# A 2x2 block product by seven quarter products in the up-projection of a gated feed-forward layer, with the activations split at the down-projection

## The chip, the cores and the metric

One core of a Trainium2 chip. The time is the device time of one execution in microseconds. The profile is one further execution of the same program, taken by the hardware profiler. In its rows PE is TensorE, DVE is VectorE, ACT is ScalarE, POOL is GpSimd and SP the queue that issues most transfers.

## The reference

Two decoder layers on x of 512 tokens and 1024 channels, in float32: a mixer and a layer norm, then a gated feed-forward block and another layer norm. The change concerns the feed-forward block alone:

```
def conv_ffn(x, w_up, conv_w, conv_b, w_down):
    h = causal_dwconv(x @ w_up, conv_w, conv_b)
    val, gate = jnp.split(h, 2, axis=-1)
    return (jax.nn.silu(gate) * val) @ w_down
...
    for layer in range(DEPTH):
        ...
        f = conv_ffn(x, ffn_w_up[layer], ffn_conv_w[layer], ffn_conv_b[layer], ffn_w_down[layer])
        x = layer_norm(ALPHA * x + f, ln2_g[layer], ln2_b[layer])
```

D_FF is 2816, so w_up is 1024 x 5632 and w_down 2816 x 1024. The convolution is depthwise over time, with three taps.

## The kernel before

Precision. TensorE multiplies in fp32r. Each float32 operand is split into a high part, which is the operand rounded to fp32r, and a low part, the difference. A product is the sum of three: high x high, low x high, high x low. `split` (L284 to L286) makes the high part on ScalarE and the low part on VectorE, or on GpSimd where the call says so.

Up-projection. `ffn` goes over 22 channel groups j of 128 channels. For each group there is a block of weights for the gate and one for the value, 128 x 1024 floats or 512 KB each: eight sub-blocks of 128 x 128, one for each 128 channels of the input. `mtile` loads and splits a block (`wload`) and runs `mpass`: 24 matmuls with 512 columns (all tokens), three passes over eight sub-blocks, into one PSUM tile. `conv` then applies the three taps: ScalarE starts with scale and bias out of PSUM (L979), and VectorE adds the two shifted taps, reading PSUM and SBUF (L981). The gate goes through Silu (L988), VectorE multiplies (L990), and the result h is split into high and low part (low part on GpSimd). All 44 parts of h stay in SBUF.

Down-projection. `proj_ln` forms h x w_down with tokens on the partitions. It goes over 11 pairs b of groups, twice: once for each half of the 1024 output channels. A step b loads a block of weights and runs 24 matmuls with 512 columns, six for each of four token tiles (L330). In the second half the last four pairs (`nres`) stay loaded, and `last(t)` finishes one token tile after the other, so that the layer norm of a tile can begin. In layer 1 the last token tile is cut into two parts of 256 columns (`parts`).

Buffers. Weight blocks have a ring of four raw buffers (`raw`) and a ring of five pairs of high and low parts (`hi`, `lo`). PSUM has eight tiles: four `mm`, two `S`, one `tp`, one `av`. Feed-forward pools (`f0`, `f1`) are opened when the mixer's pool is closed, and the other way round.

Order. A planner of the language (a list of instructions for each engine, ordered by readiness and program order) sets the order on each engine; only the places named by the kernel (`issue_after`, the `Weave` class for the mixers) add to it. Nothing in the feed-forward stage is ordered by hand.

## Time and profile before

| | |
|---|---|
| runs | median 1183.83 us of 3 (1181.13 to 1184.2) |
| the profiled execution | 1183.14 us, span 1181.3 us, granted TensorE clock 0.993 |
| TensorE busy | 1156.3 us (98%) |
| VectorE busy | 691.6 us (59%) |
| ScalarE busy | 466.7 us (40%) |
| GpSimd busy | 193.7 us (16%) |

The span is what the profile covers; the time of the profiled execution is 1.8 us longer. Busy times of TensorE include the pipelining of its matmuls, so 98% busy doesn't mean that each matmul runs at the engine's peak.

### The profile page before, as it was taken

The numbers are of one execution on the slowest core, as the hardware profiler recorded it, in microseconds if no ns is written. First come the engines' busy times: TensorE is split into PE (matmuls) and PEld (weight loads), VectorE is DVE, ScalarE is ACT, GpSimd is POOL, SyncE is SP. The second block draws the span as 40 slices with busy tenths as digits, with TensorE's granted clock in tenths as the row PEclk, the third lists the DMA queues.
The fourth block names the chain that finished last, engine by engine and source line by source line (L and its number), as shares of the span: only waits on it lengthen the run. The fifth ranks groups of instructions, "written<-read, shape, count | busy, mean of one in ns | idle before, by whom it ended". The sixth has DMA issues, their size and how long they took to land.

```text
span 1181.3 us, 13893 instructions
## 1 busy us (share of the span) xinstructions
PE 1156.3 (98%) x5312; PEld 941.3 (80%) x5312; DVE 691.6 (59%) x1098; ACT 466.7 (40%) x715; POOL 193.7 (16%) x234
## 2 busy tenths in 40 slices
PE   8999999999999999999998999999999999999997
PEld 6867778887888888888887866687888888888886
DVE  5987756477555555542338888768555455542326
ACT  5445653224444444431214466614444444432110
POOL 1122222211101110100003048112110111110002
PEclk9999999999999999999999999999999999999999
DMA  8331341213222232233222242213222322242201
GB/s 301 111 108 72 108 158 58 98 45 133 99 91 105 89 107 90 103 130 106 90 72 81 89 143 90 98 63 107 91 105 90 107 90 101 96 139 93 96 30 72
DMA packets 37570, 119.79 MB, mean 101 GB/s; under 512 B 4200, under 2 KB 4840, under 8 KB 37504
## 3 DMA queue, kind: packets, MB, share of 16 engines
q1 hardware_dynamic: 37344, 118.38, 28.9%
q8 instruction: 42, 0.69, 0.2%
q0 software_dynamic: 160, 0.52, 0.2%
q14 instruction: 24, 0.20, 0.1%
HBM read 116.75 MB, written 2.15 MB: 101 GB/s over the span
## 4 chain that ended last, share of the span: by engine, by line
PE 91%; DVE 6%; POOL 1%; issue 1%; ACT 1%; DMA 0%; POOLq 0%; SPq 0%; DVEq 0%; ACTq 0%
PE mm L238 53%; PE mm L330 14%; PE S L330 7%; PE tp L330 3%; PE av L330 2%; PE mm L278 1%; PE S L261 1%; PE mm L427 1%; PE av L852 1%; DVE lo L286 1%; PE av L550 1%; DVE xk L411 1%; PE S L634 1%; PE tp L650 1%; PE tp L536 1%
## 5 line engine op out<-in xcount | busy, mean ns | idle before, releaser
L238 PE MATMUL mm<-xT,hi 128*128 128x512 f32 (+1 forms) x1984 | 491.3, 395 | 0.5 <-ACT xT L285 0.5
L238 PEld LDWEIGHTS mm<-xT,hi 128*128 128x128 f32 x1984 | 371.0, 189 | 80.1 <-issue 4.4
L286 DVE TENSOR_TENSOR lo<-raw,hi 128x1024 fp32r<-128x1024 f32 (+1 forms) x201 | 234.5, 1171 | 174.5 <-ACT hi L285 174.3
L285 ACT ACTIVATE hi<-raw 128x1024 fp32r<-128x1024 f32 (+1 forms) x203 | 202.3, 999 | 205.4 <-PE mm L330 133.7
L981 DVE SCALAR_TENSOR_TENSOR tmp<-mm,col,tmp 128x510 f32<-128x510 f32 (+1 forms) x176 | 131.3, 749 | 207.9 <-ACT tmp L979 205.0
L238 PE MATMUL mm<-xT,lo 128*128 128x512 f32 (+1 forms) x992 | 249.4, 390 | 0.0
L238 PEld LDWEIGHTS mm<-xT,lo 128*128 128x128 f32 x992 | 185.0, 188 | 38.6 <-issue 1.9
L286 POOL TENSOR_TENSOR h<-tmp,h 128x512 fp32r<-128x512 f32 x44 | 57.7, 1311 | 433.4 <-ACT h L285 433.4
L979 ACT ACTIVATE tmp<-mm,col 128x512 f32<-128x512 f32 x88 | 68.4, 779 | 129.7 <-PE mm L238 128.4
L330 PE MATMUL mm<-hi,h 128*128 128x512 f32 (+1 forms) x396 | 118.0, 378 | 0.0
L330 PEld LDWEIGHTS mm<-hi,h 128*128 128x128 f32 x396 | 73.6, 188 | 13.7
L330 PE MATMUL mm<-lo,h 128*128 128x512 f32 (+1 forms) x198 | 74.8, 378 | 0.0
L314 POOL TENSOR_SCALAR small<-small 128x1 f32<-128x1 f32 (+2 forms) x25 | 14.5, 580 | 341.0 <-DVE small L404 279.5
L285 ACT ACTIVATE h<-tmp 128x512 fp32r<-128x512 f32 x44 | 27.8, 632 | 100.1 <-DVE tmp L990 100.1
L330 PE MATMUL S<-hi,h 128*128 128x512 f32 x176 | 56.9, 390 | 0.0
L330 PEld LDWEIGHTS mm<-lo,h 128*128 128x128 f32 x198 | 37.3, 188 | 6.8
L330 PE MATMUL mm<-hi,T 128*128 128x512 f32 x128 | 42.4, 399 | 0.0
L285 ACT ACTIVATE xT<-mm 128x512 fp32r<-128x512 f32 x24 | 13.5, 596 | 66.6 <-PE mm L427 66.4
L988 ACT ACTIVATE tmp<-tmp 128x512 f32<-128x512 f32 x44 | 27.9, 633 | 28.8 <-DVE tmp L981 28.8
L330 PEld LDWEIGHTS S<-hi,h 128*128 128x128 f32 x176 | 33.1, 188 | 6.7
L330 PE MATMUL S<-lo,h 128*128 128x512 f32 x88 | 34.3, 390 | 0.0
L411 DVE SCALAR_TENSOR_TENSOR xk<-xk,small,tmp 128x512 f32<-128x512 f32 (+1 forms) x33 | 29.0, 922 | 6.0 <-POOL small L315 6.0
(233 smaller groups left out, 1236.2 us busy)
## 6 DMA issues: line engine op xcount, KB each, us to landing
raw<-in_W SPq DMA_DIRECT2D x190, 512.0 KB, 3.5
bc<-dr SPq DMA_DIRECT2D x20, 256.0 KB, 3.9
tmp<-in_rows SPq DMA_DIRECT2D x16, 256.0 KB, 4.0
raw<-in_W SPq DMA_DIRECT2D x8, 256.0 KB, 5.7
xk<-in_x SPq DMA_DIRECT2D x4, 512.0 KB, 5.8
tmp<-in_xT SPq DMA_DIRECT2D x7, 256.0 KB, 6.3
out<-xk SPq DMA_DIRECT2D x7, 256.0 KB, 2.0
kc<-in_consts SPq DMA_DIRECT2D x1, 352.0 KB, 6.2
```

The costliest lines, as they stand in the source:

```text
L238: T.matmul(o[:, :cols_], w[:, k * P:(k + 1) * P], xs_(xcur, part, k)[:, :cols_], start=n == 0, stop=n == 3 * NK - 1)
L261: T.matmul(os[t], xs_(xcur, part, k)[:, t * P:(t + 1) * P], w[:, sl], start=k == 0 and n == 0, stop=k == NK - 1 and n == 2)
L278: T.matmul(os[t], xs_(xcur, part, k)[:, t * P:(t + 1) * P], w[:, kk * 512:(kk + 1) * 512], start=b == 0 and kk == 0 and n == 0, stop=b == ...
L285: A.activation(hi, src, AF.Copy)
L286: (lo_eng or V).tensor_tensor(lo, src, r32(hi), ALU.subtract)
L314: G.tensor_scalar(dst, var, EPS, None, ALU.add)
L330: T.matmul(o[:, c], a[:, t * P:(t + 1) * P], ww[:, kk * 512 + c.start:kk * 512 + c.stop], start=first and kk == 0 and n == 0, stop=fin and ...
L411: V.scalar_tensor_tensor(z[:, c], z[:, c], rs, shift[h][:, c], ALU.mult, ALU.add)
L427: T.transpose(tp[:, k * P:(k + 1) * P], z[:, k * P:(k + 1) * P], ident)
L979: A.activation(c, o, AF.Identity, bias=c1(cb + j), scale=c1(cw + 2 * 2 * NJ + j))
L981: V.scalar_tensor_tensor(c[:, d:], o[:, :S - d], c1(cw + (2 - d) * 2 * NJ + j), c[:, d:], ALU.mult, ALU.add)
L988: A.activation(gt, gt, AF.Silu)
```

## The change

The up-projection of groups 0 and 1 stays. The other 20 groups are taken two at a time by `up_seven`. For a group, the gate block A and the value block B together with x form a 2x2 block product: the 1024 input channels are cut into two halves, the 512 tokens into two halves. The four quarters of the result (gate and value, left and right tokens) come from seven products of quarter size in place of eight: each is three passes over four sub-blocks with 256 columns, 12 matmuls (`mul`). For this, sums of weight blocks are formed for each group on GpSimd before they are split (`t`, and in place in `ra` and `rb`: four of 512 columns a group), and sums of quarters of x once a layer (E, S2, S3, S4, on VectorE and GpSimd). A pair of groups has seven splits of 1024 columns (one of them in two halves) instead of four; one low part is on GpSimd. The products are put together in SBUF tiles `g` and `v` by eight copies on ScalarE and eight sums of 256 columns on VectorE a pair; the convolution then reads `g` and `v`.

The product of gate and value moves from VectorE to GpSimd and is kept unsplit (`act`). The down-projection splits it where it is used, in both halves of the output, with the low part on GpSimd (`two`), in a ring of 11 tiles. That ring's pool (`dn`) is opened when the up-projection's pool (`up`) is closed.

The diff, without the lines of `proj_ln` that only pass `w` on:

```diff
--- before.py
+++ after.py
@@ -318,14 +318,18 @@
 
 
         nonlocal xcur
+        two = acts if callable(acts) else lambda b: [acts[k] for k in korder[2 * b:2 * b + 2]]
         npair = len(korder) // 2
         nres = min(4, npair)
         st = [rp.tile([P, 4, 6], F32, tag="st", name=nm("st"), bufs=4) for _ in range(NT)]
 
-        def mm(o, t, b, w, first, fin, c=slice(0, 512)):
-            hi, lo, _ = w
-            for kk in range(2):
-                ah, al = acts[korder[2 * b + kk]]
+        def pieces(b, at):
+            hi, lo, _ = wload(at + b)
+            return hi, lo, two(b)
+
+        def mm(o, t, w, first, fin, c=slice(0, 512)):
+            hi, lo, ab = w
+            for kk, (ah, al) in enumerate(ab):
                 for n, (a, ww) in enumerate(((ah, hi), (ah, lo), (al, hi))):
                     T.matmul(o[:, c], a[:, t * P:(t + 1) * P], ww[:, kk * 512 + c.start:kk * 512 + c.stop],
                              start=first and kk == 0 and n == 0, stop=fin and kk == 1 and n == 2)
@@ -351,13 +355,16 @@
             return nxt is None and t == NT - 1
 
         for b in range(npair):
-            w = wload(blk + b)
             if needs:
+                w = wload(blk + b)
                 wv.need(*needs[b])
+                w = (*w[:2], two(b))
+            else:
+                w = pieces(b, blk)
             if b % half == 0:
                 os = [ps(spare[t] if b else "mm") for t in range(NT)]
             for t in range(NT):
-                mm(os[t], t, b, w, b % half == 0, b % half == half - 1)
+                mm(os[t], t, w, b % half == 0, b % half == half - 1)
             if b % half == half - 1:
                 for t in range(NT):
                     zed(t, 0, os[t], b)
...
@@ -972,9 +979,9 @@
 
     def ffn(pool, layer, up, dn, last):
         cw, cb = C_FW[layer], C_FB[layer]
-
-        def conv(j, m):
-            o = mtile(up + m)
+        act = [pool.tile([P, 2, S], F32, tag="a", name=nm("a"), bufs=NJ // 2) for _ in range(NJ // 2)]
+
+        def conv(j, o):
             c = tmp()
             A.activation(c, o, AF.Identity, bias=c1(cb + j), scale=c1(cw + 2 * 2 * NJ + j))
             for d in range(1, 3):
@@ -982,17 +989,128 @@
                                        ALU.mult, ALU.add)
             return c
 
-        acts = []
-        for j in range(NJ):
-            gt = conv(NJ + j, 2 * j)
+        def gated(j, g, v):
+            gt = conv(NJ + j, g())
             A.activation(gt, gt, AF.Silu)
-            vl = conv(j, 2 * j + 1)
-            V.tensor_tensor(vl, vl, gt, ALU.mult)
-            hi = pool.tile([P, S], F32R, tag="h", name=nm("h"), bufs=2 * NJ)
-            lo = pool.tile([P, S], F32R, tag="h", name=nm("h"), bufs=2 * NJ)
-            split(vl, hi, lo, G)
-            acts.append((hi, lo))
-        proj_ln(acts, list(range(NJ)), dn, 2 * layer + 1, None if last else OD)
+            vl = conv(j, v())
+            G.tensor_tensor(act[j // 2][:, j % 2, :], vl, gt, ALU.mult)
+
+        with tc.tile_pool(name=f"up{layer}", bufs=1, side="left") as work:
+            up_seven(work, up, gated)
+        after_ln[:] = [None, 0]
+        with tc.tile_pool(name=f"dn{layer}", bufs=1, side="left") as work:
+            def two(b):
+                hi, lo = (work.tile([P, 2, S], F32R, tag="s", name=nm("s"), bufs=11) for _ in range(2))
+                split(act[b], hi, lo, G)
+                return [(hi[:, i, :], lo[:, i, :]) for i in range(2)]
+            proj_ln(two, range(NJ), dn, 2 * layer + 1, None if last else OD)
+
+    def up_seven(pool, up, gated):
+
+
+
+        L, R = slice(0, 256), slice(256, 512)
+
+        def quarter(h, t):
+            return [xcur[2 * part + h][:, :, t] for part in range(2)]
+
+        A11, A12, A21, A22 = quarter(0, L), quarter(1, L), quarter(0, R), quarter(1, R)
+
+        def wide():
+            return pool.tile([P, 4, 256], F32, tag="t", name=nm("t"), bufs=2)
+
+        def pair():
+            return [pool.tile([P, 4, 256], F32R, tag="o", name=nm("o"), bufs=6) for _ in range(2)]
+
+        def total(eng, d, terms):
+
+            eng.tensor_tensor(d, r32(terms[0][1][0]), r32(terms[1][1][0]), ALU.add if terms[1][0] > 0 else ALU.subtract)
+            for sign, a in ((terms[0][0], terms[0][1][1]), (terms[1][0], terms[1][1][1])):
+                eng.tensor_tensor(d, d, r32(a), ALU.add if sign > 0 else ALU.subtract)
+
+        def more(eng, d, s, a, op):
+            eng.tensor_tensor(d, s, r32(a[0]), op)
+            eng.tensor_tensor(d, d, r32(a[1]), op)
+
+        gated(0, lambda: mtile(up), lambda: mtile(up + 1))
+        e, s2 = wide(), wide()
+        total(V, e, [(1, A22), (-1, A21)])
+        E, S2, S3 = pair(), pair(), pair()
+        split(e, *E)
+        more(V, s2, e, A11, ALU.add)
+        A.activation(S2[0], s2, AF.Copy, scale=-1.0)
+        V.scalar_tensor_tensor(S2[1], s2, -1.0, r32(S2[0]), ALU.mult, ALU.subtract)
+        gated(1, lambda: mtile(up + 2), lambda: mtile(up + 3))
+
+        def wsplit(parts, lo_eng=None):
+            hi = wp.tile([P, D], F32R, tag="hi", name=nm("hi"), bufs=5)
+            lo = wp.tile([P, D], F32R, tag="lo", name=nm("lo"), bufs=5)
+            n = D // len(parts)
+            for i, p in enumerate(parts):
+                split(p, hi[:, i * n:(i + 1) * n], lo[:, i * n:(i + 1) * n], lo_eng)
+            return hi, lo
+
+        def mul(o, w, half, a, start=True):
+            n = 0
+            for ww, part in ((w[0], 0), (w[1], 0), (w[0], 1)):
+                for k in range(4):
+                    T.matmul(o[:, L], ww[:, half * 512 + k * P:half * 512 + (k + 1) * P], a[part][:, k, :],
+                             start=start and n == 0, stop=n == 11, skip_group_check=not start)
+                    n += 1
+
+        for j0 in range(2, NJ, 2):
+            js = (j0, j0 + 1)
+            ra, rb, tt, wA = [], [], [], []
+            for j in js:
+                ra.append(wraw())
+                nc.sync.dma_start(ra[-1], W[up + 2 * j])
+                rb.append(wraw())
+                nc.sync.dma_start(rb[-1], W[up + 2 * j + 1])
+            for i in range(2):
+                wA.append(wsplit([ra[i]]))
+            for i in range(2):
+                t = pool.tile([P, D], F32, tag="t", name=nm("t"), bufs=2)
+                G.tensor_tensor(t[:, 0:512], ra[i][:, 0:512], rb[i][:, 0:512], ALU.add)
+                G.tensor_tensor(t[:, 512:], t[:, 0:512], rb[i][:, 512:], ALU.add)
+                G.tensor_tensor(ra[i][:, 512:], ra[i][:, 512:], t[:, 512:], ALU.add)
+                tt.append(t)
+            if j0 == 2:
+                more(G, s2, s2, A12, ALU.subtract)
+                total(G, e, [(1, A11), (-1, A21)])
+                split(e, *S3)
+                S4 = A21
+                split(s2, *S4)
+            for i in range(2):
+                G.tensor_tensor(rb[i][:, 0:512], rb[i][:, 0:512], rb[i][:, 512:], ALU.add)
+            g = [pool.tile([P, S], F32, tag="g", name=nm("g"), bufs=3) for _ in js]
+            v = [pool.tile([P, S], F32, tag="v", name=nm("v"), bufs=3) for _ in js]
+            x = [ps("S") for _ in js]
+            for i in range(2):
+                mul(x[i], wA[i], 0, A11)
+                A.activation(g[i][:, L], x[i][:, L], AF.Copy)
+                o = ps()
+                mul(o, wA[i], 1, A12)
+                V.tensor_tensor(g[i][:, L], g[i][:, L], o[:, L], ALU.add)
+            w = wsplit([ra[0][:, 512:], ra[1][:, 512:]])
+            for i in range(2):
+                o = ps(("tp", "av")[i])
+                mul(o, w, i, A22)
+                A.activation(g[i][:, R], o[:, L], AF.Copy)
+            y = [ps() for _ in js]
+            for i in range(2):
+                w = wsplit([tt[i]], (V, G)[i])
+                mul(y[i], w, 0, E)
+                A.activation(v[i][:, R], y[i][:, L], AF.Copy, scale=-1.0)
+                mul(x[i], w, 1, S2, False)
+                A.activation(v[i][:, L], x[i][:, L], AF.Copy)
+            for i in range(2):
+                w = wsplit([rb[i]])
+                mul(x[i], w, 0, S3, False)
+                V.tensor_tensor(g[i][:, R], g[i][:, R], x[i][:, L], ALU.add)
+                V.tensor_tensor(v[i][:, R], v[i][:, R], x[i][:, L], ALU.subtract)
+                mul(y[i], w, 1, S4, False)
+                V.scalar_tensor_tensor(v[i][:, L], v[i][:, L], -1.0, y[i][:, L], ALU.mult, ALU.subtract)
+                gated(js[i], lambda: g[i], lambda: v[i])
 
     with tc.tile_pool(name="ev", bufs=1, side="left") as pool:
         even_mixer(pool)
```

## Rows read from the trace of the kernel before

**Rows 1.** The page, part 1: busy us, share of the span, instructions of each engine.

```profile
PE 1156.3 (98%) x5312; PEld 941.3 (80%) x5312; DVE 691.6 (59%) x1098; ACT 466.7 (40%) x715; POOL 193.7 (16%) x234
```

**Rows 2.** The chain in order of time, layer 0: start us, us, what.

```profile
284.11 228.52 PE mm L238 x1008
512.62 59.84 PE mm L330 x264
```

**Rows 3.** Window: us; busy of PE, PEld, DVE, ACT, POOL; PE's clock; DMA share; GB/s.

```profile
284.00:512.00 228.00, 228.00 (x1007) 188.91 (x1007) 124.35 (x149) 100.82 (x128) 27.04 (x21) 1.00 0.28 98
```

**Rows 4.** The chain at the last output tile of layer 1, 256 columns.

```profile
1116.75 0.71 PE av L330 x6
1117.47 0.72 PE mm L330 x6
```

**Rows 5.** Groups by line and shape: out<-in, xcount | busy us, mean ns | idle before.

```profile
L286 DVE TENSOR_TENSOR lo<-raw,hi 128x1024 fp32r<-128x1024 f32 x177 | 218.8, 1236 | 170.3 <-ACT hi L285 170.1
L285 ACT ACTIVATE hi<-raw 128x1024 fp32r<-128x1024 f32 x177 | 186.6, 1054 | 198.8 <-PE mm L330 133.4 <-PE av L330 39.7 <-issue 9.2
...
L979 ACT ACTIVATE tmp<-mm,col 128x512 f32<-128x512 f32 x88 | 68.4, 779 | 129.7 <-PE mm L238 128.4 <-PE mm L211 1.4
L981 DVE SCALAR_TENSOR_TENSOR tmp<-mm,col,tmp 128x511 f32<-128x511 f32 x88 | 65.8, 750 | 205.0 <-ACT tmp L979 205.0
...
L286 POOL TENSOR_TENSOR h<-tmp,h 128x512 fp32r<-128x512 f32 x44 | 57.7, 1311 | 433.4 <-ACT h L285 433.4
...
L988 ACT ACTIVATE tmp<-tmp 128x512 f32<-128x512 f32 x44 | 27.9, 633 | 28.8 <-DVE tmp L981 28.8
...
L286 DVE TENSOR_TENSOR lo<-raw,hi 128x512 fp32r<-128x512 f32 x24 | 15.8, 685 | 4.2 <-ACT hi L285 4.2
...
L340 DVE SCALAR_TENSOR_TENSOR xk<-xk,mm 128x512 f32<-128x512 f32 x20 | 13.4, 682 | 1.7 <-PE mm L330 1.3
...
L191 POOL TENSOR_TENSOR lo<-raw,hi 128x1024 fp32r<-128x1024 f32 x3 | 7.0, 2347 | 0.0
...
L540 ACT ACTIVATE wt<-tp 128x256 f32<-128x256 f32 x8 | 3.0, 370 | 0.1
```

**Rows 6.** Timeline of the odd mixer: start us, us, engine, line, operation, [idle before].

```profile
713.24 1.03 POOL L919 TENSOR_TENSOR pl<-pl 128x511 f32<-128x511 f32 x1
713.24 1.58 DVE L841 SCALAR_TENSOR_TENSOR wj<-cb,ce,wj 128x512 f32<-128x512 f32 x1
...
714.82 1.03 POOL L919 TENSOR_TENSOR pl<-pl 128x510 f32<-128x510 f32 x1
714.83 1.97 DVE L841 SCALAR_TENSOR_TENSOR wj<-cb,ce,wj 128x384 f32<-128x384 f32 x2
...
716.27 1.41 POOL L919 TENSOR_TENSOR pl<-pl 128x508 f32<-128x508 f32 x1
...
716.72 2.05 DVE L286 TENSOR_TENSOR lo<-raw,hi 128x1024 fp32r<-128x1024 f32 x1
```

**Rows 7.** Timeline some 15 us later, the same columns.

```profile
729.25 0.80 DVE L904 TENSOR_SCALAR tmp<-tp,col 128x512 f32<-128x512 f32 x1
729.33 1.03 POOL L919 TENSOR_TENSOR pl<-pl 128x510 f32<-128x510 f32 x1
...
732.24 1.28 POOL L286 TENSOR_TENSOR T<-tmp,T 128x512 fp32r<-128x512 f32 x1
732.33 1.21 DVE L896 TENSOR_TENSOR T<-T,pl 128x4 f32<-128x4 f32 x1
```

**Rows 8.** Timeline where layer 0's feed-forward pool gives way to the odd mixer's.

```profile
635.87 0.35 POOL L726 TENSOR_SCALAR hc<-col 128x40 f32<-128x40 f32 x1 [3.47 <-PE av L330]
```

**Rows 9.** The chain before layer 1's up-projection.

```profile
811.39 2.85 DVE xk L411
...
816.25 6.28 PE mm L238 x24
```

**Rows 10.** Windows: the same stretch, columns as in rows 3.

```profile
815.00:823.00 8.00, 8.00 (x36) 6.61 (x35) 6.12 (x9) 4.76 (x8) 0.00 (x0) 0.84 0.69 242
```

More of the change, by code (lines that the diff above doesn't have):

```diff
@@ L372, in proj_ln @@
         for b in range(npair - nres):
-            w = wload(blk + npair + b)
+            w = pieces(b, blk + npair)
             for t in range(NT):
                 for o, c in parts if fine(t) else [(os[t], slice(0, 512))]:
-                    mm(o, t, b, w, b == 0, False, c)
-        ws = [wload(blk + npair + b) for b in range(npair - nres, npair)]
+                    mm(o, t, w, b == 0, False, c)
+        ws = [pieces(b, blk + npair) for b in range(npair - nres, npair)]
         xnew = None if nxt is None else new_xT()
@@ L383, in last @@
                     for i, b in enumerate(range(npair - nres, npair)):
-                        mm(o, t, b, ws[i], b == 0, b == npair - 1, c)
+                        mm(o, t, ws[i], b == 0, b == npair - 1, c)
                     zed(t, 1, o, npair - 1, c)
@@ L391, in last @@
                     o = os[t]
-                mm(o, t, b, ws[i], b % half == 0, b % half == half - 1)
+                mm(o, t, ws[i], b % half == 0, b % half == half - 1)
                 if b % half == half - 1:
```

## The prediction

> **What bounds the kernel now.** I read the page first: TensorE is busy 98% of the span, VectorE 59%, ScalarE 40%, GpSimd 16% [rows 1]. Then the chain in order of time: the up-projection is one unbroken run of 1008 matmuls in 228.52 us, and the down-projection follows it in the same microsecond, without a gap [rows 2]. So a 512-column matmul costs 228.52 / 1008 = 0.2267 us, a block of 24 costs 5.44 us, and one channel group j (gate and value block) 10.88 us. The changed loop works on two groups at a time; I call that a pair: 21.76 us now, 10 pairs a layer, 20 in all. In that stage the window view shows VectorE busy 124 of 228 us, ScalarE 101, GpSimd 27 [rows 3]: nothing but TensorE has to be fast there, and ACT and DVE work several blocks ahead of it.
>
> **TensorE's part of the change.** Seven products of 12 matmuls with 256 columns stand in place of 48 with 512: 84 a group, 168 a pair. The trace has this shape: in the last output tile, six 256-column matmuls take 0.71 to 0.72 us [rows 4], 0.119 us each, with a weight load for each. So a pair needs 168 x 0.119 = 20.0 us of TensorE against 21.76. If nothing else binds, 20 x 1.76 = 35 us are saved. Groups 0 and 1 stay as they are.
>
> **What the pair asks of the others.** Durations are from [rows 5].
> - ScalarE: six 1024-wide high parts and two 512-wide (a 512-wide one taken like the 0.63 activation), 6 x 1.05 + 2 x 0.63 = 7.6; eight copies of 256 columns out of PSUM at 0.37 = 3.0; four convolution starts at 0.78 = 3.1; two Silu at 0.63 = 1.3. Sum 15.0 us, below 20: not the bound.
> - VectorE: five low parts of 1024 (1.236), two of 512 (0.685), eight convolution steps (0.75), and eight sums of 256 columns that read PSUM. The last shape isn't in the trace. From 512 to 1024 columns a low part grows by 0.551 us, so a column costs 1.076 ns, and the 512-column sum with PSUM (0.682) comes down to about 0.41; 0.682 itself is the upper bound. Sum 6.2 + 1.4 + 6.0 + 3.3 = 16.9 us (19.1 with the bound).
> - GpSimd: eight weight sums of 512, two products gate x value of 512, one low part of 1024 (2.35). A 512-column sum with fp32 output takes 1.03 undisturbed [rows 6], and the fp32r one 1.31 [rows 5]. With 1.03: 10.3 + 2.35 = 12.7 us.
> - Removed: the product on VectorE and the splitting of h (0.63 on ScalarE, 1.31 on GpSimd) per group; these are already absent from the sums.
> - DMA: four blocks of 512 KB a pair as before, at a DMA share of 0.28 [rows 3]. The weight ring has four buffers and the second block of each group is now held until late, but it is wanted late as well (products 11 to 14); priced at nothing, covered by the four splits that run ahead of TensorE, some 11 us.
>
> Taken one by one every engine is under 20 us, and the change would win. The rows of another stage say that VectorE and GpSimd can't be taken one by one.
>
> **The shared access of VectorE and GpSimd.** In the odd mixer both work on SBUF at once [rows 6]. A VectorE operation that reads two SBUF operands and meets a GpSimd sum is lengthened: a step of 512 columns takes 1.58 instead of 0.75, and a low part of 1024 2.05 instead of 1.24, by 0.83 and 0.81 [rows 5, 6]. GpSimd is lengthened in its turn: 1.41 instead of 1.03. A VectorE operation of four columns takes 1.21 us because a GpSimd operation of 1.28 runs [rows 7]. An operation with one operand in PSUM isn't touched: 0.80 beside a GpSimd sum of 1.03 [rows 7]. So the two take turns. Today the up-projection hardly shows this, since its convolution reads PSUM and GpSimd has one operation a group. After the change g and v are assembled in SBUF, so the eight convolution steps read two SBUF operands too.
>
> The price of a turn: from 713.24 to 718.77 us [rows 6] the two engines alternate without a pause, 5.53 us for three GpSimd sums and 512 + 2 x 384 + 1024 = 2304 columns of VectorE. Those cost 2304 x 1.076 = 2.48, so three sums cost 3.05, 1.02 each. By the lengthening it is 0.83 or less. I take 0.93, between the two. A pair then holds the access for: VectorE 5 x 1024 + 10 x 512 = 10,240 columns, 11.0 us; GpSimd 10 x 0.93 + 2.2 (the 2.35 less what a turn hides) = 11.5 us. Together 22.5 us (21.5 by 0.83, 23.6 by 1.02), already more than TensorE's 20.0 and the old 21.76. The eight PSUM sums of VectorE (3.3 us) can run during a GpSimd turn, but only where one happens to be on; I add 1.3 for those that don't (bounds 0 and 3.3). The pair comes to 23.8 us, bounds 21.5 and 26.9. Against 21.76: 20 x 2.04 = **+41 us**, bounds -5 and +103.
>
> **The start of the stage.** Once a layer the operand sums E, S2, S3, S4 are made: nine 1024-wide operations on VectorE (9 x 1.1 = 9.9) and five on GpSimd (5 x 1.9 = 9.5), 19.4 us of the shared access. They run beside the four unchanged blocks (21.8 us), where four low parts (4.4), two products (1.9) and the first pair's eight sums (7.4) want it too, 13.7 us. 11 us don't fit. Half of it I count as hidden by the lead of the splits: **+5.5** a layer, bounds 0 and 11.
>
> **Up to down.** Before, h was split during the up-projection. Now the activations are split at the down-projection (22 times a layer), in a pool opened when the up-projection's is closed. A row tells what that costs: the first, 40-column tile of the next layer's pool waits 3.47 us, until the last matmul on h [rows 8], so a new pool starts when all of the old is done. After the last product there remain: a sum 0.41, a convolution start 0.78, two steps 1.5, the release; then high part 1.05 and low part 2.35 before the third matmul can run. 6.1 us in which TensorE has nothing. After such a gap TensorE's clock falls: where the chain had run over VectorE for 2.85 us, 24 matmuls then take 6.28 instead of 5.44 [rows 9], and the granted clock is 0.84 in the mean of those 8 us [rows 10], partly the lower of its two levels (1.2 and 2.4 GHz). This gap is longer; I add 1.2. **+7.3** a layer, bounds 0 (the new tiles lie where old ones are free early) and 10 (another convolution in the queue). Later splits are hidden: a step b of the down-projection lasts 5.44 us on TensorE, and needs 2.1 of ScalarE and 1.24 + 2.35 of the other two in turns. Were that cover gone, it would cost up to 22 x 2.35 = 52 us a layer. Who waits behind these splits on GpSimd are only the small variance steps of the layer norm, long after.
>
> **Sum**, against the profiled execution (1183.14 us, span 1181.3; the median of the runs is 1183.83, 0.7 us more): 1183.1 + 41 + 11 + 14.6 = **1250 us**. What a measurement of this kernel can tell from no change is about 0.3%, 3.5 us.
>
> **The rule on the shared ports.** The Trainium skill, "SBUF — State Buffer", section "Who interferes with whom", says of these two engines that the pair of ports they share is locked for a whole instruction, and that a VectorE operation with two SBUF inputs contends with GpSimd's reads. The trace agrees in kind (1.58, 2.05, 1.21); in size a lengthening of 0.83 is less than the 1.03 of a whole sum. By whole instructions the time would be that of the second rival.
>
> **Rivals.**
> - *TensorE stays the bound.* If the sums of GpSimd fall where VectorE reads PSUM or rests, the pair runs at 20.0 us: -35 + 14.6 = 1163 us, or 1148 if the gap before the down-projection is hidden as well. For it: each engine alone has room (15.0, 16.9, 12.7 of 20). Against it: 22.5 us of turns don't fit into 20. It decides where a GpSimd sum costs VectorE less than 0.68 us (20.0 - 11.0 - 2.2 over ten). Chance 0.18, faster.
> - *Turns of whole instructions, and late work behind them.* VectorE's two-SBUF operations at full length (6.2 + 1.4 + 6.0 = 13.6) and GpSimd's (12.7) one after the other: 26.3 us a pair, 20 x 4.5 = +91, with the rest +25: 1299 us. ACT's and DVE's queues are in order, so a late sum also holds back the evacuations behind it. Chance 0.15, slower.
> - *A balance.* The pair at about 21 us, where the gain just pays the gaps: within 4 us of 1183. Chance 0.06: 0.05 the same, 0.01 faster.
> - *The matmuls don't shorten.* If 84 loads in a row took the 0.188 us of a weight load each, a pair would be 31.6 us on TensorE, about 1395 us. Rows 4 speak against it. Chance 0.01.
>
> My forecast has the remaining 0.60; at its bounds it gives 1178 (-5, the ends hidden) to 1312 (+103, the ends as taken). For 8 in 10 over all cases I reach down to about the first rival: 1165 to 1300. Faster 0.18 + 0.01 = 0.19, same 0.05, slower 0.60 + 0.15 + 0.01 = 0.76.
>
> **What will show it.** Right, if in the up-projection the 256-column pitch is still 0.119 us but TensorE has gaps released by VectorE's or GpSimd's low parts; if the low part of 1024 rises from 1.24 to about 1.7 in the mean and GpSimd's sums over 1.03, while VectorE's 256-column sums from PSUM stay near 0.4; if VectorE's busy share in the pairs is 9 tenths or more; and if the first matmul of the down-projection waits some 6 us for ScalarE's and GpSimd's split. Wrong, if TensorE's run stays unbroken at about 20 us a pair, or if the low parts keep their length beside a busy GpSimd. A steady wait on weight DMA would also refute me, since I gave it nothing.

## The result and the profile after

The changed kernel takes 1360.81 us (median of four runs, 1359.35 to 1361.49) against 1182.48 us for the kernel before in the same session: a ratio of 1.1507, with a 95% interval of 1.1482 to 1.1532. That is slower, as forecast, but by 178 us and not by 67, and 61 us above the top of the range. The page's part 1, and the chain by engine:

```profile
PE 1183.5 (87%) x6752; PEld 1031.4 (76%) x6752; DVE 941.6 (69%) x1290; ACT 593.9 (44%) x961; POOL 643.7 (47%) x468
...
PE 51%; DVE 22%; POOL 13%; issue 7%; DMA 5%; ACT 2%; POOLq 0%; DVEq 0%; SPq 0%; ACTq 0%
```

Beside [rows 1], TensorE falls from 98% to 87% of the span with almost the same busy time; VectorE does 250 us more work and GpSimd 450 us more. The chain, which was TensorE for 91% in the kernel before, now runs over VectorE and GpSimd for 35%. The windows (columns as in [rows 3]) show one whole pair of the first layer, then the whole up-projection of that layer:

```profile
442.50:470.70 28.20, 22.19 (x161) 21.79 (x160) 22.07 (x24) 13.41 (x22) 18.47 (x11) 0.88 0.21 73
284.00:600.00 316.00, 241.11 (x1733) 233.91 (x1731) 232.68 (x248) 150.33 (x238) 202.27 (x118) 0.87 0.25 79
```

A pair lasts 28.2 us, against 21.76 before and 23.8 forecast; ten at this pace cost 64.4 us more a layer. The second window is cut at 600; the stage ends at 597.68, with the down-projection's first matmul, so it takes some 314 us where [rows 2] had 228.5. No engine fills the 28.2 us: VectorE, the busiest but for a TensorE at a reduced clock, is busy 22.07 of it.

The chain in order of time (start us, us, what) closes that pair into a circle:

```profile
442.50 3.49 DMA raw<-in_W
...
446.12 1.74 POOL t L1073
...
468.69 1.92 DVE lo L286
...
470.63 3.69 DMA raw<-in_W
```

A weight load is followed by GpSimd's sums, the split of the last sum, VectorE's work behind it, and the low part that gives a raw buffer back to the next pair's load, 28.13 us later.

VectorE's and GpSimd's timelines in that pair (start, duration, engine, line, operation, idle before it) show both halves of the story:

```profile
446.96 0.41 DVE L1110 TENSOR_TENSOR v<-v,S 128x256 f32<-128x256 f32 x1
452.40 0.69 DVE L286 TENSOR_TENSOR lo<-raw,hi 128x512 fp32r<-128x512 f32 x1 [5.04 <-ACT hi L285]
453.11 0.75 DVE L988 SCALAR_TENSOR_TENSOR tmp<-g,col,tmp 128x511 f32<-128x511 f32 x1
453.78 0.41 DVE L1112 SCALAR_TENSOR_TENSOR v<-v,mm 128x256 f32<-128x256 f32 x1
...
456.75 0.41 DVE L1112 SCALAR_TENSOR_TENSOR v<-v,mm 128x256 f32<-128x256 f32 x1
457.08 1.72 DVE L988 SCALAR_TENSOR_TENSOR tmp<-g,col,tmp 128x511 f32<-128x511 f32 x1
458.73 3.40 DVE L286 TENSOR_TENSOR lo<-t,hi 128x1024 fp32r<-128x1024 f32 x1
462.05 1.77 DVE L988 SCALAR_TENSOR_TENSOR tmp<-g,col,tmp 128x510 f32<-128x510 f32 x1
...
467.15 1.22 DVE L286 TENSOR_TENSOR lo<-raw,hi 128x1024 fp32r<-128x1024 f32 x1
468.28 0.41 DVE L1093 TENSOR_TENSOR g<-g,mm 128x256 f32<-128x256 f32 x1
```

```profile
450.43 1.28 POOL L1075 TENSOR_TENSOR raw<-raw,t 128x512 f32<-128x512 f32 x1
456.98 1.28 POOL L996 TENSOR_TENSOR a<-tmp,tmp 128x512 f32<-128x512 f32 x1 [5.27 <-DVE tmp L988]
458.22 2.83 POOL L286 TENSOR_TENSOR lo<-t,hi 128x1024 fp32r<-128x1024 f32 x1
461.12 2.15 POOL L1073 TENSOR_TENSOR t<-raw,raw 128x512 f32<-128x512 f32 x1
```

While GpSimd waits (up to 456.98), VectorE's convolution steps take 0.75 us; as soon as GpSimd works beside them, 1.72 and 1.77. The low part of the sum tile takes 3.40 us beside GpSimd's low part of 2.83. The sums that read PSUM (L1110, L1112) stay at 0.41. The other half is the wait: from 447.4 to 452.40 VectorE has nothing. GpSimd finishes its sums without turns, but at 1.28 each and not 1.03; the last one (L1075) releases ScalarE's high part, and that VectorE's low part. TensorE pays next (its own timeline):

```profile
456.23 1.22 PE L1057 MATMUL S<-xT,hi 128*128 128x256 f32 x4 [4.97 <-DVE v L1110]
457.25 1.05 PE L1057 MATMUL S<-xT,lo 128*128 128x256 f32 x4
458.10 1.05 PE L1057 MATMUL S<-xT,hi 128*128 128x256 f32 x4
```

After the gap of 4.97 us four matmuls start every 0.85 us, and undisturbed every 0.48 (below, at 588). The mean granted clock of the window is 0.88, so for part of the pair TensorE runs at the lower level.

Groups by form over nine pairs, to set beside [rows 5] (mean ns after the comma):

```profile
L286 DVE TENSOR_TENSOR lo<-raw,hi 128x1024 fp32r<-128x1024 f32 x35 | 49.6, 1435 | 12.4 <-ACT hi L285 12.4
L286 DVE TENSOR_TENSOR lo<-t,hi 128x1024 fp32r<-128x1024 f32 x9 | 30.6, 3402 | 0.0
```

The two ends of the stage in layer 0, on TensorE's timeline (first pair, then last products and first matmuls of the down-projection); then the chain's row for the down-projection, and a window at its start, whose clock is the 0.52:

```profile
312.69 1.22 PE L1057 MATMUL tp<-xT,hi 128*128 128x256 f32 x4 [11.73 <-ACT hi L285]
320.25 1.22 PE L1057 MATMUL av<-xT,hi 128*128 128x256 f32 x4 [4.37 <-ACT hi L285]
...
588.09 0.64 PE L1057 MATMUL mm<-xT,lo 128*128 128x256 f32 x4
588.57 0.64 PE L1057 MATMUL mm<-xT,hi 128*128 128x256 f32 x4
597.68 0.80 PE L334 MATMUL mm<-hi,s 128*128 128x512 f32 x1 [8.47 <-ACT s L285]
600.26 1.22 PE L334 MATMUL mm<-hi,s 128*128 128x512 f32 x2 [1.36 <-POOL s L286]
```

```profile
600.26 62.24 PE mm L334 x262
```

```profile
600.30:606.00 5.70, 5.70 (x14) 4.50 (x15) 0.00 (x0) 2.06 (x3) 5.70 (x3) 0.52 0.14 50
```

In the first pair TensorE waits 16.1 us in these two places; between the projections 9.8 in two places, and then it works 5.7 us at a clock of 0.52. The down-projection's last 262 matmuls take 62.24 us, where all 264 took 59.84 [rows 2].

### The profile page after: what moved, and what is told of

The parts are those of the page before. It is cut to its first block, busy times and chain, and to the rows that moved or that the text cites. A ratio compares the mean times of both kernels' runs of the same rounds, so it can differ in the third digit from the quotient of the medians.

```text
span 1359.6 us, 17605 instructions
## 1 busy us (share of the span) xinstructions
PE 1183.5 (87%) x6752; PEld 1031.4 (76%) x6752; DVE 941.6 (69%) x1290; ACT 593.9 (44%) x961; POOL 643.7 (47%) x468
## 4 chain that ended last, share of the span: by engine, by line
PE 51%; DVE 22%; POOL 13%; issue 7%; DMA 5%; ACT 2%; POOLq 0%; DVEq 0%; SPq 0%; ACTq 0%
PE mm L334 13%; PE mm L238 12%; DVE tmp L988 9%; DVE lo L286 6%; PE S L334 6%; DMA raw<-in_W 5%; PE tp L334 3%; POOL t L1073 3%; POOL raw L1075 2%; POOL t L1074 2%; PE mm L1057 2%; PE S L1057 2%; PE av L334 2%; POOL raw L1084 2%; ACT hi L285 1%
## 5 line engine op out<-in xcount | busy, mean ns | idle before, releaser
L238 PE MATMUL mm<-xT,hi 128*128 128x512 f32 (+1 forms) x704 | 186.3, 401 | 0.5 <-ACT xT L285 0.5
L238 PEld LDWEIGHTS mm<-xT,hi 128*128 128x128 f32 x704 | 129.2, 190 | 29.9 <-issue 4.4
L286 POOL TENSOR_TENSOR s<-a,s 128x1024 fp32r<-128x1024 f32 x44 | 107.3, 2446 | 92.3 <-PE mm L334 74.2
L334 PE MATMUL mm<-hi,s 128*128 128x512 f32 (+1 forms) x396 | 122.6, 390 | 19.7 <-ACT s L285 16.9
L1057 PE MATMUL mm<-xT,hi 128*128 128x256 f32 x640 | 113.2, 304 | 0.0
L1057 PE MATMUL S<-o,hi 128*128 128x256 f32 x640 | 101.2, 285 | 12.0 <-ACT v L1105 12.0
L1057 PEld LDWEIGHTS mm<-xT,hi 128*128 128x128 f32 x640 | 99.6, 215 | 0.0
L988 DVE SCALAR_TENSOR_TENSOR tmp<-g,col,tmp 128x511 f32<-128x511 f32 x80 | 93.7, 1172 | 0.3
L238 PE MATMUL mm<-xT,lo 128*128 128x512 f32 (+1 forms) x352 | 91.2, 391 | 0.0
L988 DVE SCALAR_TENSOR_TENSOR tmp<-v,col,tmp 128x511 f32<-128x511 f32 x80 | 87.3, 1092 | 0.0
L238 PEld LDWEIGHTS mm<-xT,lo 128*128 128x128 f32 x352 | 64.7, 188 | 13.8 <-issue 1.9
L1075 POOL TENSOR_TENSOR raw<-raw,t 128x512 f32<-128x512 f32 x40 | 51.4, 1284 | 37.8 <-DVE lo L286 37.8
```

What stands on the lines that cost most here:

```text
L238: T.matmul(o[:, :cols_], w[:, k * P:(k + 1) * P], xs_(xcur, part, k)[:, :cols_], start=n == 0, stop=n == 3 * NK - 1)
L286: (lo_eng or V).tensor_tensor(lo, src, r32(hi), ALU.subtract)
L334: T.matmul(o[:, c], a[:, t * P:(t + 1) * P], ww[:, kk * 512 + c.start:kk * 512 + c.stop], start=first and kk == 0 and n == 0, stop=fin and ...
L988: V.scalar_tensor_tensor(c[:, d:], o[:, :S - d], c1(cw + (2 - d) * 2 * NJ + j), c[:, d:], ALU.mult, ALU.add)
L1057: T.matmul(o[:, L], ww[:, half * 512 + k * P:half * 512 + (k + 1) * P], a[part][:, k, :], start=start and n == 0, stop=n == 11, skip_group ...
L1075: G.tensor_tensor(ra[i][:, 512:], ra[i][:, 512:], t[:, 512:], ALU.add)
```

## The experiments

Two theories stood at first. TURNS: VectorE and GpSimd lose time to each other, and that sets the pair. LOOP: the pair is a closed circle, weight load, weight sum, split, release of one of the four raw buffers, next load, and turns matter little. Every kernel below is an edit of the changed one.

**side_sums: the sums' work without their place in the chain.** GpSimd adds constant activation tiles, as many and as wide; the products take other weights, so the output is not the reference's.

```
-G.tensor_tensor(t[:, 0:512], ra[i][:, 0:512], rb[i][:, 0:512], ALU.add)
+G.tensor_tensor(t[:, 0:512], act[0][:, 0, :], act[0][:, 1, :], ALU.add)
...
-G.tensor_tensor(rb[i][:, 0:512], rb[i][:, 0:512], rb[i][:, 512:], ALU.add)
+G.tensor_tensor(tt[i][:, 0:512], tt[i][:, 0:512], act[0][:, 1, :], ALU.add)
```

> Same number and shape of GpSimd sums as in the changed kernel, but they add a constant tile into t; the splits of the other blocks read the raw weights, so the sums no longer stand between a weight transfer and a split (the output is not the reference's). Theory LOOP (the pair's 28.2 us is a closed circle through the four raw buffers: low part of the value block, transfer 3.6, sums 5.6, high part 0.6, VectorE's queue 18.9): without the sums in the circle the pair falls to what VectorE needs with its turns, 22 to 23.5 us, about 1245 to 1265 us in all. Rival TURNS (the pair is set by VectorE and GpSimd taking turns, and its idle time is only how it is spread): the turns are all still there, 27 to 28 us a pair, 1340 to 1365 us.

1326.77 us, ratio 1.124 (1.1221 to 1.1259). One pair of it, as a window:

```profile
433.15:459.50 26.35, 21.34 (x168) 20.43 (x168) 26.09 (x24) 13.31 (x22) 21.94 (x12) 1.00 0.25 81
```

VectorE now has no idle time: 26.09 of 26.35 us. The chain is worth 1.85 us a pair, the rest is VectorE's own time. The time lies between the two forecasts, nearer to TURNS.

**no_sums: the eight weight sums left out** (output not the reference's).

```
-t = pool.tile([P, D], F32, tag="t", name=nm("t"), bufs=2)
-G.tensor_tensor(t[:, 0:512], ra[i][:, 0:512], rb[i][:, 0:512], ALU.add)
...
+t = act[0].rearrange("p a b -> p (a b)")
```

> The eight weight sums of a pair are left out (splits read raw blocks and a constant tile; the output is not the reference's). LOOP: the circle and most turns are gone, TensorE's 20 us or VectorE's 17 to 19 us set the pair: 20 to 21.5 us, about 1195 to 1225 us with the ends. TURNS: about 6 us of turns less than in the changed kernel, the 6 us of VectorE's idle time stay: 22 us, about 1235 us or more. A third possibility, that 256-column matmuls themselves are the loss, would leave it above 1300 us.

1201.74 us, ratio 1.0172 (1.0156 to 1.0189). The window of a pair:

```profile
440.00:460.20 20.20, 20.20 (x169) 20.06 (x168) 18.77 (x24) 13.26 (x22) 6.24 (x3) 1.00 0.33 103
```

TensorE sets the pace, close to the 20.0 us that the prediction gave it. This is LOOP's number (1195 to 1225 us) and not TURNS's (1235 or more): VectorE's 6 us of idle time go with the sums too. The eight sums alone are worth 8 us a pair, or 159 us of time. Yet the kernel is still 20 us slower than before: the ends of the stage cost more than the products save.

**raw8: the ring opened.** Pairs 2, 4 and 6 load into activation tiles that are not yet in use, so eight raw buffers serve the first seven pairs.

```
+late = [a.rearrange("p a b -> p (a b)") for a in act[7:]] if j0 in (4, 8, 12) else None
-ra.append(wraw())
+ra.append(late[2 * len(ra)] if late else wraw())
...
+rb.append(late[2 * len(rb) + 1] if late else wraw())
```

> The 2nd, 4th and 6th pair of a layer load their weights into four activation tiles that are written only later, so that up to the 7th pair there are eight raw buffers instead of four; nothing else changes. LOOP: in those pairs the transfer and the sums run a pair ahead, the pair falls to 22 to 24 us in about six of ten, 12 x 5 = 60 us less, about 1290 to 1310 us. TURNS: buffers don't matter, 1350 to 1365 us.

1365.7 us, ratio 1.1559 (1.1542 to 1.1576): no gain. The total hides that the second pair of each layer takes 41.1 us here (VectorE's last sum of a pair starts at 337.90, then at 379.00); the opened pairs 3 to 6 settle at 27.20 us each, 1 us less than in the changed kernel, where LOOP said 22 to 24. So the circle through the raw buffers isn't the main cause. The window of such a pair:

```profile
410.00:437.20 27.20, 22.49 (x170) 22.17 (x170) 25.39 (x24) 13.53 (x22) 21.49 (x12) 0.87 0.24 78
```

VectorE's busy time went from 22.07 to 25.39 us: the sums that used to run while VectorE was idle now meet it. What the wait gives back, the turns take. And another circle closes, through GpSimd's queue:

```profile
426.81 0.63 ACT L285 ACTIVATE hi<-raw 128x512 fp32r<-128x512 f32 x1 [7.77 <-POOL raw L1076]
...
433.63 1.30 POOL L996 TENSOR_TENSOR a<-tmp,tmp 128x512 f32<-128x512 f32 x1 [5.63 <-DVE tmp L988]
```

GpSimd's 21.49 us of work run in one piece; the last sums release ScalarE's high parts, VectorE's work behind those releases GpSimd's next product, for which GpSimd has stood still for 5.63 us. The run excludes one circle, not circles as such.

**onepool: the down-projection's split tiles reuse the up-projection's tiles** instead of a new pool.

```
-with tc.tile_pool(name=f"dn{layer}", bufs=1, side="left") as work:
-    hi, lo = (work.tile([P, 2, S], F32R, tag="s", name=nm("s"), bufs=11) for _ in range(2))
+    tg, n = (("t", 2), ("o", 6), ("o", 6), ("o", 6))[b % 4]
+    hi, lo = (work.tile([P, 2, S], F32R, tag=tg, name=nm("s"), bufs=n) for _ in range(2))
```

> The down-projection's split activations take the buffers of the up-projection's own pool (eight tiles by tag) instead of a new pool of eleven that opens when the old one closes. If the 8.5 us in which TensorE waits for the first split are the release of the whole old pool: 8 to 11 us less a layer, about 1338 to 1345 us. If they are the up-projection's late tail itself: no change, 1355 to 1362 us.

1344.09 us, ratio 1.1376 (1.1357 to 1.1396), 8.4 us a layer less, as forecast for the release of the whole old pool. The down-projection's first 18 matmuls now run right behind the last product. The wait that is left, 2.58 us in place of 9.8, comes after them and is for VectorE's last sum out of PSUM:

```profile
589.86 0.40 PE L334 MATMUL mm<-hi,s 128*128 128x512 f32 x1
...
596.72 0.79 PE L334 MATMUL mm<-hi,s 128*128 128x512 f32 x1 [2.58 <-DVE v L1113]
```

**v_sums: the same sums on VectorE**, in all four lines.

```
-G.tensor_tensor(t[:, 0:512], ra[i][:, 0:512], rb[i][:, 0:512], ALU.add)
+V.tensor_tensor(t[:, 0:512], ra[i][:, 0:512], rb[i][:, 0:512], ALU.add)
...
```

> The eight weight sums of a pair of groups are issued on VectorE in place of GpSimd; same sums, same place in the chain. TURNS (the two engines lose time to each other): VectorE's own work is then 16.9 + 8 x 0.69 = 22.4 us a pair (a 512-column operation of two operands takes 685 ns in the kernel before), and what GpSimd keeps, two products and one low part, leaves some 2 to 4 us of conflict, so 24 to 26 us a pair in place of 28.2 and a time of about 1275 to 1305 us. Rival (GpSimd's sums are simply slow and late, and the two engines do not hinder each other): VectorE flat at 22.4 us a pair, 1245 to 1260 us. If VectorE's total is what counts and the conflict is worth less than the 5.5 us of added work, the time would not fall below that of the changed kernel.

1285.53 us, ratio 1.0868 (1.0845 to 1.0892). This is what TURNS forecast (1275 to 1305 us, 24 to 26 a pair). Giving the busier engine more work, 5.5 us by the estimate, makes the pair shorter. Three pairs, 24.8 us each, and one such sum in the chain:

```profile
394.08:468.53 74.45, 66.17 (x501) 63.18 (x501) 70.65 (x94) 41.61 (x65) 20.10 (x9) 0.95 0.26 82
...
409.47 0.60 DVE t L1073
```

VectorE is busy 23.55 us a pair.

**side_memset: GpSimd busy, but not reading.** Four fills a group in place of the four sums (output not the reference's).

```
-G.tensor_tensor(t[:, 0:512], ra[i][:, 0:512], rb[i][:, 0:512], ALU.add)
...
+for n in range(3):
+    G.memset(t, 0.5 * n)
...
+G.memset(tt[i], 1.5)
```

> The eight weight sums are left out (the products then take the wrong weights, so the output is not the reference's) and GpSimd writes constants instead: three fills of the whole 1024-column sum tile and one more for each half of a pair, which read nothing. TURNS as a matter of GpSimd's reads: VectorE keeps its own 17 to 19 us, TensorE sets the pair at 20.2 to 21.5 us as in the run without sums, 1200 to 1225 us. Rival (any work of GpSimd lengthens VectorE's): 25 to 26 us a pair as in the run with the sums on the side, 1290 to 1325 us.

1213.07 us, ratio 1.0261 (1.0245 to 1.0276). A pair, and the fills in two pairs:

```profile
361.35:381.64 20.29, 20.29 (x170) 20.20 (x170) 18.93 (x24) 13.32 (x23) 13.17 (x12) 1.00 0.34 104
...
L1074 POOL MEMSET t<- 128x1024 f32 x11 | 10.1, 953 | 0.2
```

GpSimd works 7 us more than without sums, and VectorE's 18.93 us are close to the 18.77 of no_sums. It is the sums' reading, not GpSimd's activity, that lengthens VectorE's work.

**no_start: GpSimd's five operand sums left out** at the start of the stage (output not the reference's).

```
-more(G, s2, s2, A12, ALU.subtract)
-total(G, e, [(1, A11), (-1, A21)])
```

> GpSimd's five sums that make the third and fourth activation operands at the start of each layer's stage are left out (the splits take the tiles as they are, so the output is not the reference's). If the first pair's waits on TensorE (11.7 and 4.4 us a layer) come from these sums standing ahead of the weight sums on GpSimd's queue: 10 to 15 us a layer, about 1330 to 1340 us. If the pace of the later pairs takes it back: 1352 to 1361 us.

1333.81 us, ratio 1.1278 (1.1259 to 1.1297): 13.5 us a layer. TensorE's waits of 11.73 and 4.37 us become:

```profile
301.04 0.74 PE L1057 MATMUL tp<-xT,hi 128*128 128x256 f32 x4 [1.52 <-ACT hi L285]
...
307.40 1.23 PE L1057 MATMUL av<-xT,hi 128*128 128x256 f32 x4 [4.01 <-ACT hi L285]
```

**down_only: the old up-projection**, and of the change only the unsplit activations with their splits at the down-projection, and the product on GpSimd.

```
-up_seven(work, up, gated)
+for j in range(NJ):
+    gated(j, lambda: mtile(up + 2 * j), lambda: mtile(up + 2 * j + 1))
```

> The old up-projection, a group at a time with eight 512-column matmuls each, and of the change only the unsplit activations with their splits at the down-projection, the pool of their tiles, and the product on GpSimd. If the splits are hidden behind TensorE and only the release of the old pool costs, and that is short because the up-projection's last work is short: within 10 us of the kernel before, 1181 to 1192 us. If the splits at the down-projection cost by themselves: 1195 to 1215 us.

1181.84 us, ratio 0.9997 (0.9988 to 1.0006). The down-projection is again 59.84 us in one run of the chain, right behind the last product:

```profile
499.86 12.69 PE mm L238 x56
512.55 59.84 PE mm L334 x264
```

So the splits are hidden, and the new pool costs nothing where GpSimd and VectorE are not behind when it opens.

**dma_sums: the sums by transfers that add at their destination**, on top of onepool; no engine computes them.

```
-G.tensor_tensor(t[:, 0:512], ra[i][:, 0:512], rb[i][:, 0:512], ALU.add)
...
+for h in range(2):
+    nc.sync.dma_start(t[:, h * 512:(h + 1) * 512], wa[:, 0:512])
+for h in range(2):
+    G.dma_start(t[:, h * 512:(h + 1) * 512], wb[:, 0:512], accum_op=ALU.add)
+G.dma_start(t[:, 512:], wb[:, 512:], accum_op=ALU.add)
+G.dma_start(ra[i][:, 512:], t[:, 512:], accum_op=ALU.add)
...
```

> The eight weight sums of a pair are made by transfers that add to what stands at their destination (GpSimd issues five a group; the sum tile's two halves are loaded by plain transfers first), so no compute engine makes them; the down-projection's split tiles reuse the up-projection's tiles as in the run with one pool. TURNS: with GpSimd's sums gone VectorE keeps 17 to 19 us a pair and TensorE sets it at 20.2; 1201.7 us of the run without sums, less 16.7 for the pool, less some of the 27 that the operand sums at the start cost, as they no longer stand ahead of weight sums: 1160 to 1190 us. Rival (issuing the transfers, or three that must follow one another, takes longer than a pair's 20 us, or TensorE waits for them): 24 us a pair or more, 1220 us or more.

1460.5 us, ratio 1.236 (1.234 to 1.2381). Two of the page's groups of transfers that GpSimd issues:

```profile
L1079 POOL DMA_DIRECT2D t<-in_W x40 | 35.4, 886 | 154.6 <-DMA t<-in_W 143.5
L1089 POOL DMA_DIRECT2D raw<-in_W x40 | 37.9, 948 | 93.0 <-DMA raw<-in_W 74.5
```

The rival was right: GpSimd's queue stands still 3.9 and 2.3 us before each, mostly until the transfer ahead has landed. The wait has only changed its owner.

**combo: no_sums, onepool and no_start together** (output not the reference's).

> Three cuts at once: no weight sums, no operand sums by GpSimd at the start of the stage, one pool for both projections (the output is not the reference's). It bounds what the seven products could give here if TensorE alone set the stage. If the three costs add: 1201.7 - 16.7 - 27.0 = 1158 us, some 2% under the kernel before, where the matmuls alone allow 35 us (1148). If the start costs little once the sums are gone, since TensorE then waited only for them: 1180 to 1187 us.

1160.32 us, ratio 0.9828 (0.9808 to 0.9848). The three costs nearly add (1158 forecast). With the weight sums, the five operand sums and the new pool gone altogether the change is worth 1.7%. The two runs that make correct sums without a compute engine, dma_sums and the next one, don't come near it, and no version of the seven products that computes the reference's output was found that beats the kernel before.

**ahead: sums for a whole layer made in HBM beforehand**, by plain and adding transfers during the stages in front, on top of onepool.

```
+for d, (q, h) in zip(sums[c], ((0, 0), (0, 0), (0, 1), (1, 0))):
+    nc.sync.dma_start(d, src(c, q, h))
...
+G.dma_start(d, a, accum_op=ALU.add, max_dma_last_dim=2048)
...
+nc.sync.dma_start(tt[i][:, 0:512], s[0][i])
+nc.sync.dma_start(tt[i][:, 512:], s[1][i])
...
```

> The weight sums of a whole layer are made in HBM before its stage begins: plain transfers lay down the blocks, adding transfers (issued by GpSimd, two groups each, a few at each weight load of the mixer before it, and of the down-projection and the second mixer for the second layer) put the sums on them, and the stage loads finished sums; one pool for both projections as before. TURNS: the pair runs at TensorE's 20.2 us, and the time comes near the run with three cuts (1160 us), plus what the operand sums at the start still cost: 1160 to 1180 us, faster than the kernel before. Rival (the adding transfers, some 1 us of GpSimd each and twice the bytes, hold up the mixers or the weight loads): 1200 us or more, with the loss before 284 us and between 560 and 850 us of the span.

1961.41 us, ratio 1.6599 (1.6571 to 1.6627). The rival was right, far beyond its number: the copies from HBM to HBM hold SP's queue, behind which the weight loads stand. One copy is issued every 11.2 us in the mean, and the next weight load only behind the seventh, as SP's timeline shows:

```profile
60.40 78.54 SPq L191 DMA_DIRECT2D sm<-in_W  x7
139.05 12.71 SPq L217 DMA_DIRECT2D raw<-in_W  x1
```

TURNS missed in the stage itself as well: with no weight sums on GpSimd a pair of the second layer still took 23.92 us and not 20.2, while VectorE was busy 17.50 us of it. What held it there stays open.

**side_half: as side_sums with four sums a pair**, to test an account fitted to the runs above.

```
 G.tensor_tensor(t[:, 0:512], act[0][:, 0, :], act[0][:, 1, :], ALU.add)
 G.tensor_tensor(t[:, 512:], t[:, 0:512], act[0][:, 1, :], ALU.add)
-G.tensor_tensor(t[:, 512:], act[0][:, 0, :], t[:, 512:], ALU.add)
-G.tensor_tensor(tt[i][:, 0:512], tt[i][:, 0:512], act[0][:, 1, :], ALU.add)
```

> As the run with the sums on the side (GpSimd adds constant tiles, nothing of the weight chain waits for it, the products take other weights so the output is not the reference's), but with four sums a pair in place of eight. Account FULL (VectorE spends all of its own instructions at their whole length, and each GpSimd sum adds 0.92 us to that): 18.8 us as measured without sums + 4 x 0.92 = 22.5 us a pair, 1201.7 + 20 x 2.3 = 1247 us, between 1240 and 1255. Account COLUMNS (as predicted: only the columns of VectorE's two-operand work and GpSimd's sums share the access, the rest overlaps): 11.0 + 6 x 0.93 + 2.2 + 1.3 = 20.1 us, so TensorE sets the pair at 20.2 and the time is 1200 to 1212 us.

1275.79 us, ratio 1.0798 (1.078 to 1.0816), over both forecasts. The window, and ScalarE's wait in it:

```profile
371.53:395.70 24.17, 21.83 (x169) 21.63 (x169) 22.76 (x24) 13.31 (x22) 13.56 (x8) 0.93 0.28 88
...
375.18 1.06 ACT L285 ACTIVATE hi<-raw 128x1024 fp32r<-128x1024 f32 x1 [5.34 <-DMA raw<-in_W]
```

VectorE's busy time, 22.76, is what FULL said (22.5) and COLUMNS excluded. But the pair is 1.4 us longer than VectorE's work, since a weight load starts only when VectorE's late low part has released its raw buffer, as in the changed kernel's chain. As a time for the pair FULL fails too: VectorE's total is a lower bound, and the wait for the load adds to it.

## Why the prediction was wrong

**TensorE** was right: four 256-column matmuls every 0.48 us, and 20.2 us a pair where nothing else binds. The rival "the matmuls don't shorten" is out.

**The mechanism** was right in part. VectorE and GpSimd do lose time to each other (v_sums, side_memset), VectorE's sums out of PSUM keep their 0.41 us, and the low parts of 1024 columns rise to 1.82 us in the mean of both kinds (80.2 us for 44), where the sign was about 1.7. But a pair is not only the time for which the shared access is held. VectorE was to be busy 9 tenths of the pair and was busy 78%. And the sign that would refute me, a steady wait on weight DMA, is in the chain of every pair (442.50, 470.63).

**The step that failed is the pair, 23.8 us, which came out as 28.2**, by two parts:
- *The overlap credited to VectorE's own work, 2.5 us.* I let it hold the access for 11.0 us by its columns alone, and 1.3 of 3.3 us for PSUM sums, 12.3 in all. The timelines give, from start to start and undisturbed, 1.13 us for a low part of 1024 columns (467.15 to 468.28), 0.63 for one of 512 (side_half), 0.66 for a step and 0.33 for a sum out of PSUM (456.75 to 457.08): 5 x 1.13 + 2 x 0.63 + 8 x 0.66 + 8 x 0.33 = 14.8 us, all of it spent. The prices of GpSimd's share were right: by no_sums, products and low part cost VectorE 18.77 - 14.8 = 4.0 (forecast 1.9 + 2.2 = 4.1); by side_sums, the eight sums cost 26.09 - 18.77 = 7.3, or 0.92 each (forecast 0.93). These three add up to side_sums' 26.1 because they are taken from it. Two other runs test them: v_sums, 14.8 + 4.0 + 8 x 0.60 = 23.6 against 23.55 us, and side_half, 22.5 against 22.76.
- *The wait that was priced at nothing, 1.85 us.* I took the pair to be as long as the shared access is in use. In the changed kernel the sums stand in a chain, load, sum, high part, low part, and VectorE idles 6.1 us behind it; sums that run meanwhile cost it no turns, so only 28.20 - 26.35 = 1.85 us is lost on balance. I had called the raw ring covered by the splits that run ahead. More buffers don't cure it (raw8). How the 1.85 us divides between chain and TensorE's lower clock after each gap is open, and so is any one split of the 4.4: the 2.5 and 1.85 are taken with side_sums as the yardstick, while in the changed kernel itself VectorE works 22.07 us of a pair and waits for 6.1.

So the second rival's 26.3 us a pair was nearer than my forecast, but by luck: it counts both engines' two-operand work too long (13.6 and 12.7 us, against 12.2 and 11.3) and the sums out of PSUM, 2.6 us, at nothing. A GpSimd sum costs VectorE 0.92 us, less than its length of 1.28.

**GpSimd's own time** was undersized: 1.28 us a sum in this stage without VectorE beside it, against 1.03 from [rows 6]. I called those undisturbed, though a VectorE step of 1.58 us starts with the first of them. Why the sums of this stage take longer stays open. It matters here because they are in the chain. A small slip in the turns' upper bound changes nothing: by the terms as stated, 11.0 + 10.2 + 2.2, it is 23.4 and not 23.6.

**The start**, +5.5 with bounds 0 and 11, measured 13.5 a layer by no_start. I added up the work and credited the lead of the splits; but the first pair's weight sums stand behind GpSimd's operand sums in one queue, and these five took 14.7 us where I had 9.5. GpSimd's timeline from the last of them on:

```profile
302.87 3.20 POOL L1033 TENSOR_TENSOR t<-t,xT 128x1024 f32<-128x1024 f32 x1
306.03 1.27 POOL L1073 TENSOR_TENSOR t<-raw,raw 128x512 f32<-128x512 f32 x1
...
310.71 1.26 POOL L1075 TENSOR_TENSOR raw<-raw,t 128x512 f32<-128x512 f32 x1
```

When that L1075 ends, TensorE's wait of 11.73 us ends too, after ScalarE's high part.

**Up to down**, +7.3 with bounds 0 and 10: from the end of the last product at 589.2 to the end of the down-projection's run at 662.5 it takes 73.3 us, where 59.84 were enough before. That is 13.4 us, 9.8 of them waiting and the rest a start at half clock. The release of the whole old pool was the right reason (onepool takes back 8.4). "Later splits are hidden" was right (down_only).

**The ledger** of a layer: 64.4 + 13.5 + 13.4 = 91.3 us; twice that is 183, against the 178 measured, so the parts overlap a little. By them 20 x 4.4 = 88 us of what I missed are the pair, 16 the start and 12 the way to the down-projection: 116, where 111 were missed.

## What to carry to other kernels

An engine's account is its instructions from start to start, all of them, plus what a neighbour on its shared access costs; don't credit overlap for fixed parts and PSUM reads that the trace has not shown to overlap. Work that moves to a free engine is not free if it reads through a shared access, or if it stands between a load and its first use: price both, and expect that removing one wait can feed the other, as in raw8. A saving of 8% in one engine's time (20.0 for 21.76 us) leaves little to pay with, so add up the ends of the stage first; here they alone took back more than it gave.

## What the runs showed of the hardware

A VectorE low part of 1024 columns takes 3.40 us beside a GpSimd low part of 2.83 that began 0.5 us earlier, 2.2 more than alone; it ends 1.08 us after the other, little less than the 1.22 that it takes alone. GpSimd's fills of the same tile (0.95 us each) left VectorE's busy time of a pair at 18.93 us, against 18.77 without them. This agrees with the Trainium skill, "SBUF — State Buffer", section "Who interferes with whom", where a VectorE instruction with two SBUF inputs contends with a GpSimd instruction that reads SBUF and not with one that only writes.

In dma_sums, adding transfers of 256 KB from HBM land after 5.7 us in the median, and GpSimd spends 0.9 to 1.2 us on issuing each. In ahead, seven copies of 512 KB from HBM to HBM held SP's queue for 11.2 us each in the mean.
